# An RWKV time-mixing kernel: adding the mixes of two units in one instruction, and issuing the last three staged loads one unit sooner

## The chip, the cores and the metric

The kernel runs on one core of a Trainium2 chip. The metric is the device time of one execution in microseconds (us), as the median of several runs. Beside it there is a profile of one execution, taken by the hardware profiler; its span runs from the first to the last instruction of the program.

The engines are named as in the profile: PE is the matrix engine (PEld its weight loads), DVE the vector engine, ACT the scalar engine, POOL the GpSimd engine, SP the engine that issues most DMAs. POOL and ACT issue some DMAs too.

## The reference

The input is `x`, 16 batches of 2048 tokens with 256 features, in float32. For each token the kernel mixes it with the token before it, projects the mix twice, and combines the two results:

```
x_prev[:, 1:] = x[:, :-1]                 # zero at the first token of a batch
xv = x * time_mix_v + x_prev * (1 - time_mix_v)
xr = x * time_mix_r + x_prev * (1 - time_mix_r)
v  = xv @ value_weight                    # 256 x 256
r  = xr @ receptance_weight               # 256 x 256
out = (sigmoid(r) * v) @ output_weight    # 256 x 256, float32
```

The reference also makes a mix and a projection for `k`, but its output doesn't use them, and the kernel leaves them out.

## The kernel before

**Units.** The 16 x 2048 tokens are cut into NU = 64 units of 512 tokens, four to a batch. In the transposed layout (features on the partitions) a unit's mix is a tile of 128 x 1024 bf16. The kernel folds `time_mix` into the weights, so that a mix is `c * x_prev + x` with one factor `c = 1/time_mix - 1` per feature: a scaling, and then an add. `m = 0` stands for the receptance mix and `m = 1` for the value mix. The features are held as two halves, `ko = 0` and `ko = 1`.

**The loop.** The main loop runs over g = 0 to 62. Its iteration g does, for unit g, on PE: `project(ps_r, g, 0)` (four matmuls into `psum_r`), the eight transposes of unit g + 6 into `ps_t` while units are still transposed on PE (up to unit 39), `project(ps_v, g, 1)` (four matmuls into `psum_v`), and `output` for an earlier unit (eight matmuls into `psum_o`). For g above 32 the output belongs to unit g - 2 and stands ahead of the value projection. ACT takes the sigmoid of `psum_r` into `s_sb`, copies the transposes out and copies `psum_o` to the output tile. DVE multiplies `s_sb` by `psum_v` into `z_sb`. In what follows r(g), v(g), o(g) are the three groups of matmuls of unit g, and z(g) is that multiplication. `psum_v` has one buffer only (`bufs=1`), so v(g + 1) can't begin until z(g) has read v(g).

**The mixes.** They are made ahead of the projections. From unit 10 (`PAIRS`) on the scaling is done for two units at once (128 x 1024 for one half of the features): DVE scales `ko = 0` (`scale`, L334), POOL scales `ko = 1` (`scale_pool`, L344), and late in the kernel ACT scales `ko = 0` of the value mixes (`scale_act`, L609). The add is done unit by unit on DVE (`add`, L356, 128 x 1024). The lists `products`, `pooled`, `sums` and `held`, built at L577 to L604, say what each iteration issues. DVE's order in iteration g is: the scaling in `products[g]`, the adds in `sums[g]`, z(g), the adds in `held[g]`. Before the change `sums[g]` holds the add of the value mix of unit g + 1, and `held[g]`, behind z(g), the add of the receptance mix of unit g + 2. POOL's scaling in iteration g is made to wait for the last add of `sums[g]`:

```
        for p in pooled[g]:
            wrap_slots(p, after=last)
            scale_pool(p, last)
```

**Order.** The program order is the one written: the kernel turns the automatic scheduling off, and each engine executes its instructions in that order. `wrap_slots` copies one slot of the transposed tile (L528) at each fourth unit.

**Loads and transposes.** Units 0 to 39 (batches 0 to 9) are loaded with a cast to bf16 and transposed on PE. Batches 10 to 15 are staged as bf16 in DRAM (`x_natural`), by loads on POOL's queue, and come into SBUF by two DMA transposes on SP's queue, `by_dma` (L251): batches 10 to 12 at g = 27, batches 13 to 15 at g = 39 (`T_AT`). The loads of batches 13, 14 and 15 are issued at the end of the iterations in `STAGE_AT`, behind POOL's scaling of that iteration. They wait until the first DMA transpose has landed; the second one waits for the last of them. Some stores are held back so that they don't run beside a transpose (`FIRST`, `WAITING`). A store of two units is 1 MB.

Of the kernel before, what the change touches and what calls it, by code (L numbers as in the profile page):

```python
# [15 lines left out]
def kernel(  # L16
# [32 lines left out]
    TU = UJ * P  # L49
# [8 lines left out]
    CROSS = NU - BYDMA - LOOK  # L58
# [3 lines left out]
    FIRST = {21: 27, 27: 39, 29: 39}  # L62
    WAITING = {23: 27, 25: 27, 31: 39, 33: 39, 35: 39}
    ZEROS_AT = 12
    STAGE_AT = {33: 13, 34: 14, 35: 15}
    GROUPS = [(2, 3), (4, 5, 6), (7, 8, 9), (10, 11, 12), (13, 14, 15)]
    HALVED = (12, 15)
    PAD = 16
# [4 lines left out]
    PAIRS = 10  # L73
# [63 lines left out]
    def zero_rows(b, k):  # L137
        rows = zeros[k * PAD : (k + 1) * PAD].rearrange("p (o c) -> p o c", o=1)
        nc.gpsimd.dma_start(
            out=x_both[b][k, :PAD].rearrange("p (h c) -> p h c", c=P),  # L140
            in_=rows.to_broadcast([PAD, KO, P]),
        )

    def load(b):
        if b < STAGED:
            x_bf[b] = xpool.tile([P, J, D], BF16, name="x_bf")
        if b < BYUNIT:
            for e in range(UB):
                nc.gpsimd.dma_start(
                    out=x_bf[b][:, e * UJ : (e + 1) * UJ, :], in_=unit_rows(x, b, e)[:, 0]  # L150
                )
            return
        if b in HALVED:
            return [
                nc.gpsimd.dma_start(out=x_bf[b][:, j : j + J // 2], in_=rows(b)[:, j : j + J // 2])
                for j in (0, J // 2)
            ]
        run = 8192 if b < LONG else 16384
        return nc.gpsimd.dma_start(out=x_bf[b], in_=rows(b), max_dma_last_dim=run)  # L159
# [339 lines left out]
    def tile_for(b):  # L499

        if b not in mix:
            mix[b] = mixpool.tile([P, 2, 2 * UJ, KO, P], BF16, name="mix")

    def pieces(g):

        b, e = divmod(g, UB)
        tile_for(g // 2)
        return [(b, m, e * TU, (e + 1) * TU) for m in range(2)]
# [68 lines left out]
    sums = {g: [] for g in range(-1, NU)}  # L577
# [4 lines left out]
    first = {}  # L582
    held[0].append(pieces(1)[1])
    pooled[0].append(pieces(1)[1])
    for u in range(2, NU):
        p0, p1 = pieces(u)
        if u - 1 <= AHEAD:
            sums[u - 1].append(p0)
        else:
            held[u - 2].append(p0)  # L590
        (held if u - 1 < AHEAD else sums)[u - 1].append(p1)
        first[u] = (u - 1 if u - 1 <= AHEAD else u - 2, u - 1)
# [24 lines left out]
    for g in range(NU - 1):  # L617
# [48 lines left out]
        n = TU // 2 if g == NU - 2 else TU  # L666
# [10 lines left out]
        if ZEROS_AT <= g < ZEROS_AT + len(pads):  # L677
            zero_rows(*pads[g - ZEROS_AT])
        if g in STAGE_AT:
            b = STAGE_AT[g]  # L680
            loads[b] = load(b)
# [40 lines left out]
```

## Time and profile before

| what | value |
|---|---|
| median of 3 runs | 200.81 us (199.84 to 201.69) |
| profiled execution, its own time | 201.01 us |
| span of the profile | 199.2 us |
| PE busy | 192.5 us (97%) |
| DVE busy | 184.4 us (93%), 289 instructions |
| ACT busy | 177.0 us (89%) |
| POOL busy | 86.9 us (44%) |
| DMA | 58.13 MB, mean 292 GB/s |
| DVE adds `mix<-mix,xt_both` (L356), 128 x 1024 | 112, 701 ns each |
| DVE multiplications z (L668), 128 x 1024 | 62, 1216 ns each |
| POOL scalings (L344), 128 x 1024 | 54, 1122 ns each |

Busy times are unions of records. The records of neighbouring instructions on one engine overlap by some tens of ns, so the time that an instruction takes up on its engine is read from the start of one to the start of the next, which is shorter than its record. A busy PE isn't PE at its peak, and an idle gap matters only on an engine that others wait for.

### The profile page before, as it was taken

The page shows a single profiled execution, that of the slowest core. Times are in us where ns is not written, and L with a number is a line of the kernel's source. Part 1 is how long each engine was busy: PE and PEld are TensorE (multiplying, and loading weights), DVE is VectorE, ACT ScalarE, POOL GpSimd, SP SyncE. Part 2 cuts the span into 40 slices and gives each one's busy share as a digit, 9 for nine tenths or more (in the row PEclk, how much of TensorE's full clock was granted, in tenths as well). Part 3 has the DMA queues.
Part 4 walks back from the last instruction along what each step waited for, and adds up shares of the span by engine and source line. Part 5 has one row for each costly group of instructions (what it writes and reads, how often), then busy time and mean ns, then how long its engine had stood idle before and what let it go on. Part 6 is the DMA issues. An engine that isn't in the chain of part 4 may idle for free.

```text
span 199.2 us, 3758 instructions
## 1 busy us (share of the span) xinstructions
PE 192.5 (97%) x1368; PEld 123.5 (62%) x1368; DVE 184.4 (93%) x289; ACT 177.0 (89%) x197; POOL 86.9 (44%) x115
## 2 busy tenths in 40 slices
PE   8999999999999999999999999999999999999990
PEld 3555676666666666666666556666666666666660
DVE  0899999999999999999999999999999999999960
ACT  3699899999999999999999999999999999999970
POOL 1656452453675635524424366444444444444200
PEclk9999999999999999999999999999999999999998
DMA  5799999999999999999999999999999999999994
GB/s 177 203 187 215 215 280 275 278 282 274 286 312 332 285 285 331 296 268 211 296 250 290 367 276 207 209 280 295 198 238 346 416 421 400 409 399 407 409 392 177
DMA packets 37961, 58.13 MB, mean 292 GB/s; under 512 B 26068, under 2 KB 27448, under 8 KB 35128
## 3 DMA queue, kind: packets, MB, share of 16 engines
q1 hardware_dynamic: 33392, 41.34, 60.7%
q0 software_dynamic: 4400, 16.44, 41.6%
q8 instruction: 10, 0.16, 0.3%
q10 hardware_dynamic: 152, 0.13, 0.2%
q14 instruction: 7, 0.06, 0.1%
HBM read 34.34 MB, written 39.90 MB: 373 GB/s over the span
## 4 chain that ended last, share of the span: by engine, by line
PE 88%; ACT 4%; DMA 2%; issue 2%; DVE 1%; SPq 0%; DVEq 0%
PE psum_v L364 26%; PE psum_o L393 26%; PE psum_r L364 26%; PE ps_t L269 8%; DMA w_f<-n_receptance_weight_dram 2%; ACT xt_first L286 1%; ACT s_sb L629 1%; PE psum_r L378 1%; PE ps_t L393 1%; ACT mix L609 1%; ACT o_sb L442 1%; PE ps_t L364 0%; SPq L171 0%; DVE z_sb L668 0%; DVE mix L356 0%
## 5 line engine op out<-in xcount | busy, mean ns | idle before, releaser
L344 POOL TENSOR_SCALAR mix<-xt_both,c_sb 128x1024 bf16<-128x1024 bf16 (+1 forms) x55 | 61.3, 1114 | 84.7 <-DVE mix L356 82.8
L356 DVE TENSOR_TENSOR mix<-mix,xt_both 128x1024 bf16<-128x1024 bf16 x112 | 77.4, 701 | 1.4
L668 DVE TENSOR_TENSOR z_sb<-s_sb,psum_v 128x1024 bf16<-128x1024 bf16 (+1 forms) x64 | 76.7, 1200 | 1.9 <-PE psum_v L364 0.8
L364 PEld LDWEIGHTS <-w_bf 128*128 128x128 bf16 x516 | 49.0, 98 | 38.7 <-DVE mix L356 0.5
L629 ACT ACTIVATE s_sb<-psum_r 128x1024 bf16<-128x1024 f32 x63 | 65.2, 1035 | 6.2 <-PE psum_r L364 6.0
L364 PE MATMUL psum_v<-mix,w_bf 128*128 128x512 bf16 (+1 forms) x256 | 65.3, 377 | 0.1
L364 PE MATMUL psum_r<-mix,w_bf 128*128 128x512 bf16 (+1 forms) x252 | 64.2, 377 | 0.0
L393 PE MATMUL psum_o<-wo_bf,z_sb 128*128 128x256 bf16 x486 | 63.4, 273 | 0.2 <-DVE z_sb L668 0.2
L393 PEld LDWEIGHTS <-z_sb 128*128 128x128 bf16 x512 | 51.7, 103 | 18.2 <-DVE z_sb L481 0.7
L442 ACT COPY o_sb<-psum_o 128x1024 f32<-128x1024 f32 x50 | 51.2, 1024 | 5.0 <-PE psum_o L393 5.0
L286 ACT COPY xt_both<-ps_t 128x1024 bf16<-128x1024 bf16 x32 | 32.8, 1036 | 0.0
L269 PEld LDWEIGHTS <-x_bf 128*128 128x128 bf16 x304 | 19.7, 98 | 8.9 <-DMA x_bf<-in_x_dram 1.5
L269 PE MATMUL ps_t<-ident,x_bf 128*128 128x128 bf16 x304 | 22.7, 219 | 0.3 <-DMA x_bf<-in_x_dram 0.3
L334 DVE TENSOR_SCALAR mix<-xt_both,c_sb 128x1024 bf16<-128x1024 bf16 (+1 forms) x47 | 21.1, 458 | 0.0
L609 ACT ACTIVATE mix<-xt_both,c_sb 128x1024 bf16<-128x1024 bf16 x14 | 16.3, 1161 | 0.0
L356 DVE TENSOR_TENSOR mix<-mix,xt_first 128x1024 bf16<-128x1024 bf16 x15 | 10.6, 713 | 0.1
L442 ACT COPY x_bf<-psum_o 128x1024 f32<-128x1024 f32 x10 | 10.2, 1015 | 0.0
L334 DVE TENSOR_SCALAR mix<-xt_first,c_sb 128x512 bf16<-128x512 bf16 x22 | 6.5, 348 | 0.3 <-ACT xt_first L279 0.2
L286 ACT COPY xt_first<-ps_t 128x1024 bf16<-128x1024 bf16 x6 | 6.2, 1027 | 0.0
L159 POOL DMA_DIRECT2D x_bf<-in_x_dram x8 | 5.7, 712 | 0.0
L528 POOL COPY xt_first<-xt_first 128x254 bf16<-128x254 bf16 x5 | 2.0, 395 | 6.6 <-DVE mix L356 6.6
L344 POOL TENSOR_SCALAR mix<-xt_first,c_sb 128x512 bf16<-128x512 bf16 x6 | 4.1, 689 | 0.7 <-DVE mix L356 0.2
(70 smaller groups left out, 54.0 us busy)
## 6 DMA issues: line engine op xcount, KB each, us to landing
out_dram<-o_sb SPq DMA_DIRECT2D x24, 1024.0 KB, 14.1
x_bf<-in_x_dram POOLq DMA_DIRECT2D x8, 1024.0 KB, 20.6
x_natural<-in_x_dram POOLq DMA_DIRECT2D x4, 1024.0 KB, 13.3
out_dram<-x_bf SPq DMA_DIRECT2D x4, 1024.0 KB, 13.1
x_natural<-in_x_dram POOLq DMA_DIRECT2D x4, 512.0 KB, 15.2
x_bf<-in_x_dram POOLq DMA_DIRECT2D x6, 256.0 KB, 6.1
out_dram<-x_bf SPq DMA_DIRECT2D x6, 256.0 KB, 4.2
o_sb<-in_x_dram SPq DMA_DIRECT2D x4, 256.0 KB, 4.0
```

Source lines behind the costliest of these rows:

```text
L159: return nc.gpsimd.dma_start(out=x_bf[b], in_=rows(b), max_dma_last_dim=run)
L269: nc.tensor.transpose(out=ps[:, jj], in_=src[:, jj, ko * P : (ko + 1) * P], identity=idn)
L286: nc.scalar.copy(out=xt[b][:, j0 : j0 + UJ], in_=ps)
L334: nc.vector.tensor_scalar(out=mixed(piece)[:, :, ko], in0=tokens(piece, 0, ko), scalar1=c_sb[:, m, ko : ko + 1], scalar2=None, op0=ALU.mult,)
L344: op = nc.gpsimd.tensor_scalar(out=mixed(piece)[:, :, 1], in0=tokens(piece, 0, 1), scalar1=c_sb[:, m, 1:2], scalar2=1.0, op0=ALU.mult, op1 ...
L356: return nc.vector.tensor_tensor(out=mixed(piece), in0=mixed(piece), in1=tokens(piece, 1), op=ALU.add)
L364: nc.tensor.matmul(out=ps[:, mo, :], lhsT=w_bf[:, m, ko, mo * P : (mo + 1) * P], rhs=mixed((b, m, e * TU + lo, e * TU + hi))[:, :, ko], st ...
L393: nc.tensor.matmul(out=ps[:, j, :], lhsT=slot[:, ko, j], rhs=wo_bf[:, ko, :], start=(ko == 0), stop=(ko == KO - 1),)
L442: nc.scalar.copy(out=o[:, j0 : j0 + UJ, :], in_=ps)
L609: nc.scalar.activation(out=mixed(piece)[:, :, ko], in_=tokens(piece, 0, ko), func=ACT.Copy, scale=c_sb[:, m, ko : ko + 1],)
L629: nc.scalar.activation(out=s_sb, in_=ps_r, func=ACT.Sigmoid)
L668: nc.vector.tensor_tensor(out=z_sb[:, :, c : c + n], in0=s_sb[:, :, c : c + n], in1=ps_v[:, :, c : c + n], op=ALU.mult,)
```

## The change

For units 12 to 35 the adds are made for two units at once. For each even unit u in that range one add of 128 x 2048 covers the receptance mixes of u and u + 1, in `sums[u - 2]`, and one covers their value mixes, in `sums[u - 1]`. Both stand ahead of the z of their iteration; `held` gets nothing for these units. The 48 single adds of these 24 units go, and 24 double ones come, so that DVE has 24 instructions fewer. Units up to 11 and from 36 on keep the old lists.

The loads of batches 13, 14 and 15 are issued at the end of iterations 32, 33 and 34 and no longer 33, 34 and 35. On POOL's queue each thereby moves ahead of one scaling.

```diff
-    STAGE_AT = {33: 13, 34: 14, 35: 15}
+    STAGE_AT = {32: 13, 33: 14, 34: 15}
...
     for u in range(2, NU):
         p0, p1 = pieces(u)
+        if PAIRS + 2 <= u < CROSS + 2:
+            if u % 2 == 0:
+                for n, (b, m, lo, hi) in ((2, p0), (1, p1)):
+                    sums[u - n].append((b, m, lo, hi + TU))
+            first[u] = (u - 2, u - 1)
+            continue
         if u - 1 <= AHEAD:
             sums[u - 1].append(p0)
         else:
             held[u - 2].append(p0)
         (held if u - 1 < AHEAD else sums)[u - 1].append(p1)
         first[u] = (u - 1 if u - 1 <= AHEAD else u - 2, u - 1)
```

Iteration 10 stands at the border: its `sums` holds the single add of the value mix of unit 11, from the old lists, and then the double add of the receptance mixes of units 12 and 13. Iteration 34 stands at the other one: its `sums` is empty.

## The prediction

> **What bounds the kernel now.** I read first the slices of the page, then the stretches, then the timelines of DVE and PE around unit 10, where the new adds begin, and last the stores at the end.
>
> ```profile
> PE   8999999999999999999999999999999999999990
> DVE  0899999999999999999999999999999999999960
> DMA  5799999999999999999999999999999999999994
> ```
>
> PE, DVE and the DMA engines are all nearly full, so a saving on DVE alone may buy nothing. The table by stretches (busy time of PE, PEld, DVE, ACT, POOL, then the clock, the DMA share, GB/s) says how full:
>
> ```profile
> 40.00:45.00 5.00, 5.00 (x39) 3.29 (x37) 4.90 (x8) 5.00 (x6) 2.94 (x6) 1.00 1.05 281
> ...
> 112.00:134.00 22.00, 22.00 (x138) 13.31 (x136) 21.88 (x32) 20.53 (x23) 11.04 (x12) 1.00 1.01 259
> ...
> 151.00:186.00 35.00, 35.00 (x218) 22.47 (x217) 34.87 (x49) 32.56 (x35) 14.97 (x14) 1.00 1.03 405
> 186.00:199.20 13.20, 7.99 (x58) 5.16 (x56) 6.77 (x11) 6.73 (x13) 0.00 (x0) 0.93 0.82 315
> ```
>
> PE has no idle time at all from 25 us to 186 us: a unit takes 3.05 us with transposes, 2.60 us without, and no wait on DVE is left to take out. DMA is at a share of 1.0 too. At the end the DMA engines drain stores. The view of the output tensor gives, for the store issued at 171.3 us and for the last two, issued at 194.4 and 195.1 us:
>
> ```profile
> DMA to landing us min/median/max: 14.1/14.1/14.1
> ...
> DMA to landing us min/median/max: 3.0/3.0/3.0
> ```
>
> A backlog of stores shrinks towards the end and is almost gone with the last one, which is copied on DVE at 194.18 + 0.43 = 194.6, issued at 195.1 and lands at 198.1. So two limits meet there, PE and the stores.
>
> **What the Trainium skill says.** (1) "VectorE: DVE Perf Modes", section "The TRN2 errata", says that the fixed latency is paid once per instruction, so a larger tile pays it once; the table of tiers in that page keeps a bf16 `tensor_tensor` at 2 elements a cycle. The trace agrees with the fixed part: adds that follow one another start 0.60 us apart, and 1024 elements at 2 per 0.96 GHz cycle are 0.53 us. (2) "SBUF", section "SBUF: two separate sides", says that an add of two SBUF inputs on DVE and a POOL instruction that reads SBUF exclude each other for a whole instruction. The trace agrees: POOL's scaling ends at 42.54 and the add begun at 42.30 takes 0.78 us, not 0.69. (3) "Perfetto Trace Analysis", section "Matmuls", wants matmul groups to rotate through PSUM banks so that the evacuation of one overlaps the next. `psum_v` can't: one buffer. In the trace v(10) starts 0.08 us after the record of z(9) ends. (4) "DMA: Bandwidth & Descriptors", section "Anatomy of one DMA", gives a fixed 2.0 us and the bytes at 436 GB/s; as an estimate from it a store of 128 KB alone lands after 2.3 us. The last one took 3.0, so it had about 0.7 us of backlog before it.
>
> **The change part by part.**
>
> *DVE's saving.* Two adds take 2 x 0.60 = 1.20 us. A double one is not in the trace. Upper bound 1.20 (nothing shared); lower bound 1.07 (its elements alone). I take 0.53 x 2 + 0.07 = 1.13. 24 of them save 24 x 0.07 = 1.7 us of DVE. Against it stands that each double add follows the scaling it depends on: in iteration 9 such an add starts 0.58 us after the scaling (39.98 to 40.56), where an independent one starts after 0.40 (43.00 to 43.40). Before, half of the iterations pay that, now all. DVE's unit is then 0.58 + 1.13 + 1.13 (z) = 2.84, up to 0.1 for POOL's lock and 0.14 for the slot copy in each fourth unit: 2.97 against PE's 3.05. It fits, and it is worth nothing, as no PE wait ends with a DVE add there.
>
> *The border at unit 10.* Here is the cost. DVE, and then PE:
>
> ```profile
> 41.17 1.21 DVE L668 TENSOR_TENSOR z_sb<-s_sb,psum_v 128x1024 bf16<-128x1024 bf16 x1
> 42.30 0.78 DVE L356 TENSOR_TENSOR mix<-mix,xt_both 128x1024 bf16<-128x1024 bf16 x1
> 43.00 0.47 DVE L334 TENSOR_SCALAR mix<-xt_both,c_sb 128x1024 bf16<-128x1024 bf16 x1
> 43.40 0.68 DVE L356 TENSOR_TENSOR mix<-mix,xt_both 128x1024 bf16<-128x1024 bf16 x1
> 44.00 1.21 DVE L668 TENSOR_TENSOR z_sb<-s_sb,psum_v 128x1024 bf16<-128x1024 bf16 x1
> ```
>
> ```profile
> 42.46 1.03 PE L364 MATMUL psum_v<-mix,w_bf 128*128 128x512 bf16 x4
> ...
> 45.06 0.61 PE L269 MATMUL ps_t<-ident,x_bf 128*128 128x128 bf16 x8
> 45.50 1.03 PE L364 MATMUL psum_v<-mix,w_bf 128*128 128x512 bf16 x4
> ```
>
> The rows are z(9), the late add of unit 11's receptance mix, the scaling for 12 and 13, the add of unit 11's value mix, z(10). DVE is behind already: v(10) ends at 43.49 and z(10) starts at 44.00. The change puts a double add ahead of z(10), in the one iteration that still has both single adds: z(10) starts at 44.00 + 1.13 = 45.13 and ends at 46.34; v(11), due at 45.50, starts at 46.42. Behind it in PE's queue stands everything else. Cost: 0.92 us of PE, once. Nothing hides it; PE has no gap to give back.
>
> *After it.* z(10) is followed by the scaling, which POOL's lock (scaling 45.3 to 46.4) holds to 46.4, the double add at 46.98, z(11) from 48.1 to 49.3; v(12) is due at 46.42 + 3.05 = 49.47. It fits by 0.15 us, and each unit wins about 0.1 back. POOL's scaling starts when the add before it ends and takes 1.12 us, while DVE does z and a scaling (1.71), so it is ready for the next double add.
>
> *The other border, unit 34.* Iteration 34 loses its add ahead of z(34), and DVE waits for PE some 1 us. From z(35) on, the order is the old one. No gain: PE is the bound.
>
> *The loads.* Three issues of about 0.56 us each on POOL move ahead of one scaling each. Load 13 can't go before the first transpose has landed, at 99.0 + 13.7 = 112.7, against 115.0 before. POOL waits there about 1 us at most; queued behind is the scaling of iteration 33, which itself waits for an add that ends near 114, so it is hidden (if not, the add that reads it comes 3 us later). Load 14 goes from 117.8 to about 116, load 15 from 120.2 to about 118.
>
> ```profile
> 99.00 11.61 SPq L251 DMA_TRANSPOSE xt_both<-x_natural  x1
> ...
> 133.90 17.23 SPq L251 DMA_TRANSPOSE xt_both<-x_natural  x1
> ```
>
> The second transpose waits for load 15, landing at 120.7 + 13.0 = 133.7. In this stretch the DMA share is 1.01: the loads share the engines with 2 MB of stores, and an earlier issue shifts the bytes but doesn't shrink them. I take 0.3 us gained at the start of the transpose; bounds 0 and 2 (a real idle gap, which no slice shows).
>
> *The end.* PE is 0.9 later: the last copy ends at 195.5. The stores have had 0.9 us more to drain and began up to 0.3 earlier, so the 0.7 of backlog and part of the 0.46 between copy and issue go. 195.5 + 0.2 + 2.4 = 198.1 to 198.4, against 198.1. Net +0.2 us. The profiled execution's 201.01 becomes 201.2; it stood 0.2 above the median of 200.81, so the median becomes 201.0.
>
> **The rivals.**
>
> *A, the stall is passed on in full* (201.7). If a store alone takes 3.0 us anyway, the tail gives nothing back: 200.81 + 0.92. For it: the landing times at the end flatten out at 3.0. Against it: the very first load, 256 KB in an idle start (0.75 to 3.5 us), took 2.75, and 128 KB has half the bytes.
>
> *B, the loads matter* (200.1). If the transpose starts 1 to 2 us sooner, the backlog ends sooner, the tail shrinks by its 0.7, and with a smaller stall than mine the net is -0.7. Against it: the DMA share of 1.01. For more than 1% PE too would have to end 2 us sooner, and it has no idle time.
>
> *C, slower: DVE no longer fits in PE's unit* (203.6). Place: units 11 to 35. Price: if a double add costs more than 1.21 from start to start, DVE's unit exceeds 3.05 and the lag never heals; each z frees `psum_v` late. At 1.33 that is 0.12 x 23 = 2.8 on top of 0.9, less 0.9 that the tail absorbs: +2.8. It decides from about 1.29, where the sum passes 2 us. For it: the margin is only 0.08 a unit, and POOL's lock may cost more than 0.1. Against it: the fixed part is paid once.
>
> *D, the change does not do what it says*: in the changed program's own order of instructions DVE has 24 fewer, with the double adds where I put them, so this gets no chance.
>
> **How the numbers follow.** My forecast 0.60, A 0.16, B 0.14, C 0.10. 1% (2 us) is about what a measurement of this kernel can tell from no change; its three runs spread over 0.9%. My forecast, A and nearly all of B lie within 1%: same 0.86. Slower by over 1% is C, 0.10; faster is the outer end of B, 0.04. The range runs from B, 200.0, to a mild C, 202.3.
>
> **What would show it.** Right: DVE has 24 adds of 128x2048 with records near 1.22 us; PE shows one gap near 0.9 us before v(11), put down to DVE, and none later; the stretches of 15 us after it are full; load 13 is issued near 112.8, the second transpose between 133.3 and 134.5; the last stores land in less than 3.0 us. Wrong: gaps of PE before many v between 48 and 112 us (C); no gap at 45.5 us; a second transpose before 132.5 us (B); or last stores that still take 3.0 us (A).

## The result, and the profile after

| | median | range | runs |
|---|---|---|---|
| before | 201.03 us | 199.37 to 202.15 | 22 |
| after | 200.22 us | 199.64 to 201.79 | 22 |

The ratio is 0.9974 with a 95% interval of 0.9955 to 0.9993, so the change saves 0.5 us (0.1 to 0.9); the two medians of the table lie 0.8 apart, inside that interval. I had forecast 201.0, no change or 0.2 us more. The profiled execution of after took 200.22 us, with a span of 198.4 us (before 201.01 and 199.2).

The slices of the page look almost as before:

```profile
PE   8899999998999999999999999999999999999992
DVE  1899999999999999999999979999999999999972
DMA  5999999999999999999999999999999999999985
```

What is new on PE stands in the tenth slice (its 8), and DVE's idle time in the 24th (the first 7). PE's waits in all:

```profile
PE psum_r L378 <- DVE w_prev L549: 0.9, 1, 0.9
PE ps_t L201 <- PEq L712: 0.8, 1, 0.8
PE psum_v L364 <- DVE z_sb L674: 0.7, 1, 0.7
PE psum_o L393 <- DVE z_sb L674: 0.2, 1, 0.2
PE ps_t L269 <- DMA x_bf<-in_x_dram: 0.2, 1, 0.2
```

Each row gives us in total, times, and the longest. The third is the only wait on DVE in the main loop, and it comes once. The first two and the last belong to the head of the program, the fourth to its end; before has these four kinds too. The wait is the one at the border, read in the timeline of DVE and then of PE:

```profile
43.13 1.81 DVE L356 TENSOR_TENSOR mix<-mix,xt_both 128x1024 bf16<-128x1024 bf16 x2
44.87 1.21 DVE L674 TENSOR_TENSOR z_sb<-s_sb,psum_v 128x1024 bf16<-128x1024 bf16 x1
46.00 0.47 DVE L334 TENSOR_SCALAR mix<-xt_both,c_sb 128x1024 bf16<-128x1024 bf16 x1
46.58 1.23 DVE L356 TENSOR_TENSOR mix<-mix,xt_both 128x2048 bf16<-128x2048 bf16 x1
47.72 1.22 DVE L674 TENSOR_TENSOR z_sb<-s_sb,psum_v 128x1024 bf16<-128x1024 bf16 x1
```

```profile
42.19 1.03 PE L364 MATMUL psum_v<-mix,w_bf 128*128 128x512 bf16 x4
...
46.13 1.02 PE L364 MATMUL psum_v<-mix,w_bf 128*128 128x512 bf16 x4 [0.73 <-DVE z_sb L674]
```

The row "x2" of 1.81 us joins the single add and the double one, and z(10) stands behind both. v(11) was due at 42.19 + 3.05 = 45.24 and starts at 46.13, 0.9 late; the trace puts 0.73 of it down to z(10). So PE loses what I said it would. The gain is elsewhere: on SP's queue and in the stretch of the second DMA transpose. These are the rows of the transpose in after, and then the stretch of 134 to 152 us of before and of after (the columns are those of the prediction's table; the last one is GB/s):

```profile
134.25 15.31 SPq L251 DMA_TRANSPOSE xt_both<-x_natural  x1
```

```profile
134.00:152.00 18.00, 18.00 (x112) 11.54 (x111) 17.91 (x25) 16.37 (x19) 7.86 (x7) 1.00 1.18 254
```

```profile
134.00:152.00 18.00, 18.00 (x113) 11.43 (x111) 17.90 (x25) 16.37 (x18) 7.84 (x7) 1.00 1.19 288
```

The transpose starts 0.35 us later than before (134.25 against 133.90), and its issue takes 15.31 us and not 17.23. SP is free for the next store at 149.6 and not at 151.1. In the same 18 us the DMA engines move 288 GB/s and not 254, at the same busy share. That lead lasts to the end, where the last stores of after, five of them issued after 193 us, show:

```profile
L411 SPq DMA_DIRECT2D out_dram<-x_bf x4: 332/338/410, 193.7 to 195.3; - x4
...
DMA to landing us min/median/max: 2.0/2.0/2.0
```

In before the five stores issued after 193 us took 3.0 to 3.6 us, and the groups of DMA issues on the page tell the same of the larger ones: the median store of 256 KB now lands after 2.5 us, and took 4.2. So the stores are no longer behind. The last copy ends at 194.81 + 0.42 = 195.23, its store is issued at 195.26 without a wait, and lands at 197.26; before it was 194.61, 195.07 and 198.06.

### The profile page after: what moved, and what is told of

Its sections match the earlier page's. It is cut to its first block, busy times and chain, and to the rows that moved or that the text cites. A ratio compares the mean times of both kernels' runs of the same rounds, so it can differ in the third digit from the quotient of the medians.

```text
span 198.4 us, 3734 instructions
## 1 busy us (share of the span) xinstructions
PE 191.7 (97%) x1368; PEld 122.7 (62%) x1368; DVE 183.0 (92%) x265; ACT 176.9 (89%) x197; POOL 87.1 (44%) x115
## 4 chain that ended last, share of the span: by engine, by line
PE 74%; DVE 16%; issue 3%; DMA 2%; ACT 1%; POOL 1%; SPq 0%; DVEq 0%; POOLq 0%
PE psum_v L364 22%; PE psum_o L393 22%; PE psum_r L364 22%; DVE mix L356 6%; DVE z_sb L674 5%; PE ps_t L269 5%; DVE mix L334 4%; DMA w_f<-n_receptance_weight_dram 2%; PE ps_t L393 1%; PE psum_r L378 1%; ACT xt_first L279 1%; ACT s_sb L635 1%; PE ps_t L364 0%; SPq L171 0%; POOL x_bf L159 0%
## 5 line engine op out<-in xcount | busy, mean ns | idle before, releaser
L356 DVE TENSOR_TENSOR mix<-mix,xt_both 128x1024 bf16<-128x1024 bf16 (+1 forms) x88 | 72.3, 835 | 2.5
```

The source lines that it names most:

```text
L356: return nc.vector.tensor_tensor(out=mixed(piece), in0=mixed(piece), in1=tokens(piece, 1), op=ALU.add)
```

## The experiments

Every ratio below is to the kernel before, run beside the other on the same chip.

### Which part, and what sets the end

One theory (L in the texts) was that the sooner loads bring the gain, the other (S) that by themselves they don't. The first two runs do one part of the change alone: the loads alone,

```diff
-    STAGE_AT = {33: 13, 34: 14, 35: 15}
+    STAGE_AT = {32: 13, 33: 14, 34: 15}
```

> The loads of batches 13 to 15 one unit sooner, nothing else of the change. Theory L (the gain comes from the loads: they let the second DMA transpose and the stores behind it finish sooner, so that PE and not the stores sets the end; the double adds only cost 0.9 us of PE at unit 11): faster than before by 1.0 to 1.6 us, near 199.5, and faster than the changed kernel by 0.5 to 0.9 us; PE without a gap at v(11); last store landing 2.0 us after its issue. Theory S (the gain comes from the double adds, by fewer DVE instructions and so other times of instruction fetches beside the transposes): same as before, 201.0 within 0.3 us, second transpose of 16 to 17 us, last stores 3.0 us.

Measured: 201.17 us, ratio 0.9977 (0.9947 to 1.0007). The interval holds 1, so the run alone decides nothing, but a saving of more than 1.1 us it excludes. Its profile (POOL, DVE and PE around 115 us) shows a price that the loads can have without the double adds:

```profile
115.05 0.56 POOL L159 DMA_DIRECT2D x_natural<-in_x_dram  x1 [3.66 <-DVE z_sb L668]
115.65 1.12 POOL L344 TENSOR_SCALAR mix<-xt_both,c_sb 128x1024 bf16<-128x1024 bf16 x1
```

```profile
115.20 1.85 DVE L334 TENSOR_SCALAR mix<-xt_both,c_sb 128x1024 bf16<-128x1024 bf16 x1
116.97 0.68 DVE L356 TENSOR_TENSOR mix<-mix,xt_both 128x1024 bf16<-128x1024 bf16 x1
117.58 1.21 DVE L668 TENSOR_TENSOR z_sb<-s_sb,psum_v 128x1024 bf16<-128x1024 bf16 x1
```

```profile
118.84 1.02 PE L364 MATMUL psum_v<-mix,w_bf 128*128 128x512 bf16 x4 [1.10 <-DVE z_sb L668]
```

The view puts POOL's wait down to z, but load 13 is issued 0.53 us after the landing of the first transpose, as in after. That landing came late in this execution, at 114.52: in six of the 14 profiles it is recorded 2.0 us after the last packet of the transpose and not 0.5 us, and why isn't known. POOL's scaling behind the load starts 0.6 us after it, at 115.65. There it runs beside DVE's scaling, which takes 1.85 us and not 0.47. z(34) comes late and PE loses 1.1 us. So in this profile load 13 is no sooner than in before (115.00); loads 14 and 15 are 1.1 and 1.4 us sooner. In after load 13 goes at 113.15 and DVE has 1 us to spare in iteration 34, so nothing is lost.

The double adds alone, with the old loads:

```diff
+        if PAIRS + 2 <= u < CROSS + 2:
...
+            continue
```

> The double adds for units 12 to 35, with the loads at their old places. Theory L: no faster than before, 201.0 to 201.9, as PE loses 0.9 us at v(11) and the stores still end late. Theory S: as fast as the changed kernel, near 200.2, although PE loses the same 0.9 us at v(11); second transpose near 15.3 us.

Measured: 200.61 us, 0.9969 (0.9947 to 0.9991): as much as the whole change. The stall at v(11) is there (0.7 us on PE), the issue of the second transpose takes 15.92 us, and the last store lands 2.0 us after its issue. So the gain needs no sooner load, although the adds touch neither the loads nor the transposes.

What the end is worth, I tested from both sides. First a stall at the same place without the change: three extra DVE adds of 128 x 512 ahead of z(10).

```diff
+        if g == 10:
+            for n in range(3):
+                nc.vector.tensor_tensor(out=idle[:, n], in0=wo_bf, in1=wo_bf, op=ALU.add)
```

> The kernel before with three more adds of 128 x 512 on DVE ahead of z(10), into a tile that nobody reads: they make v(11) wait about 0.8 us, as the double add does in the changed kernel, and change nothing else. If the stores set the end of the kernel before (the view in both theories), PE's 0.8 us are absorbed: 201.0 within 0.3 us. If PE sets the end in most runs, it is 0.8 us slower, 201.8.

Measured: 201.56 us, 1.0027 (1.0004 to 1.0050), which is +0.5 us (0.1 to 1.0). The stall came out larger than meant, 1.44 us at v(11) in the trace, and about a third of it shows: the end takes up the rest, and the last store again lands in 2.0 us.

Then less to store: before without the 1 MB store of units 30 and 31, whose rows of the output are left unwritten. At the 405 GB/s that the prediction's table shows from 151 us on, 1 MB is about 2.6 us of the DMA engines' time.

```diff
+            elif g == 31:
+                pass
```

> The kernel before without the 1 MB store of units 30 and 31 (that part of the output is left unwritten): 2.4 us less for the DMA engines behind the second transpose, nothing less for PE. If the stores set the end of the kernel before, it falls to where PE sets it: last store landing 2.0 us after issue, 199.3 to 199.7 us, 1.3 to 1.7 faster than before. If PE sets the end, less than 0.4 us faster.

Measured: 199.58 us, 0.9909 (0.9884 to 0.9933): 1.8 us less, though PE's work is the same and the second transpose is as slow as in before (18.09 us). So the stores, not PE, set the end of before. A sum puts both together: when PE sets the end, it is the last copy of before, 194.61, plus the stall, plus 0.03 to the issue, plus 2.0. With no stall that is 196.6, 1.4 less than before's 198.06; with 0.92 it is 197.56, 0.5 less, which is what after gained. With the 1.44 of the extra adds it is 198.08, no loss; that kernel measured 0.5 (0.1 to 1.0), so the sum is good to about half a microsecond.

### Why the second transpose got shorter

The traces of the first runs held a candidate (F), an instruction fetch. The page lists, beside the queues of the kernel's own DMAs, this one:

```profile
q14 instruction: 7, 0.06, 0.1%
```

Seven packets of 8 KB. "DMA: Bandwidth & Descriptors", section "Queues, rings and completion order", of the Trainium skill says that row 14 belongs to the runtime, refills among its uses; that q14 is this row is my reading. The packet records of the trace give the times. Two of the seven change place between the kernels: 86.8 and 147.9 us in before, 93.5 and 160.7 in after; the others stay within 1.3 us. DVE's stream is the one that the change shortens (24 instructions), so I take the two for fetches of DVE's instructions; the profile doesn't name them. (The page has a second row of this kind, q8, with ten packets of 16 KB. None of them falls between the first and the last packet of the second transpose, in any of the 14 profiles.) At 147.9 the second transpose runs, at 160.7 it doesn't. Stretches of one microsecond in before:

```profile
147.00:148.00 1.00, 1.00 (x6) 0.49 (x5) 1.00 (x3) 1.00 (x2) 0.17 (x1) 1.00 1.30 297
148.00:149.00 1.00, 1.00 (x11) 0.89 (x10) 1.00 (x2) 1.00 (x2) 0.96 (x1) 1.00 1.74 110
149.00:150.00 1.00, 1.00 (x7) 0.48 (x5) 1.00 (x2) 1.00 (x2) 0.00 (x0) 1.00 0.91 205
```

A steady 290 to 297 GB/s falls to 110 and recovers: the packets of the transpose are in flight, the busy share rises to 1.74, and they don't move. In after the same stretch reads

```profile
148.00:149.00 1.00, 1.00 (x8) 0.57 (x6) 1.00 (x2) 1.00 (x2) 0.54 (x1) 1.00 1.28 290
```

The size: from packet 6000 of the transpose to packet 12000 it takes 5.29 us without such a fetch and 6.20 to 6.22 with one, in 13 of 14 profiles; in the last one the fetch falls just before packet 6000, and the same 0.9 us are missing there. So such a fetch costs the transpose 0.92 us: the eight profiles with one have such a hole, which begins within half a microsecond of the fetch's start, and the six without have none. If F is right, DVE instructions that do nothing but fill move the hole. The fills are `nc.vector.memset` of one column. In after, 23 of them bring the count nearly back:

```diff
+    FILL = {**{g: 1 for g in range(14, 33)}, 33: 4}
...
+        for n in range(FILL.get(g, 0)):
+            nc.vector.memset(idle[:, 4 * g + n : 4 * g + n + 1], 0.0)
```

> The changed kernel with 23 tiny fills of 128 x 1 on DVE (one in each of iterations 14 to 32, four in iteration 33), which nobody reads: about as many DVE instructions as the double adds took away, in slack that DVE has. Theory F (instruction fetch: with fewer DVE instructions the fetch of DVE's next 8 KB of instructions moves from inside the second DMA transpose, 147.9 us, to behind it, 160.7 us; inside, it stops the transpose for about 1 us): the fetch comes back to about 148 us, the transpose shows a hole of 0.9 to 1.0 us just after it and takes 16 us or more, and the gain over before is lost: 201.0 to 201.4. Theory L (the gain comes from the loads and the work of DVE, not from where a fetch falls): as the changed kernel, 200.2 to 200.6.

Measured: 200.63 us, 0.9974 (0.9954 to 0.9994), no loss against after. The fetch came at 149.9 and the hole from 150.4 to 151.3:

```profile
149.00:150.00 1.00, 1.00 (x9) 0.86 (x8) 1.00 (x2) 1.00 (x2) 1.00 (x1) 1.00 1.30 297
150.00:151.00 1.00, 1.00 (x6) 0.48 (x5) 1.00 (x2) 1.00 (x2) 0.06 (x1) 1.00 1.71 122
```

So the fills do move the hole, but the time missed its forecast: the last stores still landed in 2.0 us. The transpose lost 0.9 us and the stores weren't late. That fits the sum above, in which PE, with its stall, sets the end of after.

The other way round, 28 fills in before (two in each of the iterations 17 to 30) should bring the fetch ahead of the transpose, and 8 (one in each of 17 to 24) should leave it inside, as a control for the fills' own cost.

> The kernel before with 28 tiny fills of 128 x 1 on DVE, two in each of iterations 17 to 30: more instructions, no double adds, loads at their old places. Theory F: the fetch moves ahead of the second transpose, to about 132 us; no hole in it, 15 to 16 us; the end is set by PE in most runs: 199.5 to 200.3, faster than before by 0.8 to 1.5, as PE has no gap at v(11). Theory L: no faster than before.

> The control for the 28 fills: the kernel before with 8 of them, one in each of iterations 17 to 24. The fetch moves by about 4 to 5 us only, to 143 us, still inside the second transpose. Theory F: as before, within 0.4 us, with the hole near 144 us. If tiny fills help for another reason: faster by about 0.3 of what the 28 bring.

Measured: with 28 fills 200.76 us, 0.9972 (0.9944 to 1.0000), fetch at 132.9 (and an eighth packet on q14, at 193.2), no hole; with 8 fills 201.63 us, 1.0013 (0.9992 to 1.0035), fetch at 145.8 and the hole behind it at 146. But the transpose with 28 fills, expected at 15 to 16 us, was hardly shorter than in before:

```profile
134.03 17.03 SPq L251 DMA_TRANSPOSE xt_both<-x_natural  x1
```

Its first 2000 packets took 4.4 us (3.8 in before), and its last stores landed after 2.6 us or more. So the hole moves as F says and the fills cost nothing that shows, but this pair does not show that moving it saves time: the profile misses the forecast, and each interval touches 1.

### Taking the stall away

If PE sets the end of after, it should gain from a border without the stall. In this version, shown against after, no iteration near unit 10 gets a double add on top of a single one: the doubles begin at unit 16, for the value mixes first, and for the receptance mixes at unit 20; the units 16 to 19 keep single receptance adds.

```diff
-        if PAIRS + 2 <= u < CROSS + 2:
+        if PAIRS + 6 <= u < CROSS + 2:
...
-                    sums[u - n].append((b, m, lo, hi + TU))
+                    if m or u >= PAIRS + 10:
+                        sums[u - n].append((b, m, lo, hi + TU))
+            if u < PAIRS + 10:
+                (held if u % 2 else sums)[u - 2].append(p0)
```

> The changed kernel with a gentler border: double adds of the value mixes from units 16 and 17 on, of the receptance mixes from units 20 and 21 on; for units 16 to 19 the receptance mix of the even unit is added ahead of z, of the odd unit behind it. 18 DVE instructions fewer than before, loads one unit sooner. By the sum of starts z is never more than 0.5 us late, so PE has no gap on DVE between 25 and 186 us. Theory F: the fetch falls near 157 us, behind the transpose: PE's 0.9 us are won, 199.3 to 199.7. If instead the stall is not what the changed kernel loses: 200.2.

Measured: 199.85 us, 0.9949 (0.9929 to 0.9968): 1.0 us less than before, the lowest time of all that computes everything. Its interval overlaps that of after (0.9955 to 0.9993), so that it beats after is likely but not shown. From 25 to 192 us its profile has a single wait of PE:

```profile
PE psum_o L393 <- DVE z_sb L677: 0.2, 1, 0.2
```

and the transpose is the short one, 15.31 us:

```profile
133.53 15.31 SPq L251 DMA_TRANSPOSE xt_both<-x_natural  x1
```

This version has no stall to cover a late store, so it can tell what each cause of the shorter transpose is worth. Once with the old loads, and once with the new loads and 22 fills that put the fetch back into the transpose:

> The kernel with the gentler border, but the loads of batches 13 to 15 at their old places. If the loads matter for how fast the second transpose gets going (its first 1000 packets took 1.6 to 2.0 us in four profiles with sooner loads and 2.2 to 3.9 in six with old ones): 2.2 us or more for them and slower than with sooner loads by 0.3 to 0.8 us, 200.2 to 200.7. If only the double adds matter: 199.85, within 0.3 us.

> The kernel with the gentler border and sooner loads, with 22 tiny fills of 128 x 1 on DVE (one in each of iterations 16 to 32, five in iteration 33) that bring DVE's instruction fetch from 157 us back to about 147 us, into the second transpose. Theory F: a hole of 0.92 us in the transpose, whose issue takes 16.2 us, not 15.3; PE's end is at 196.3 in this kernel, so 0.2 to 0.9 us of it show in the time: 200.1 to 200.7. If the fetch costs nothing: 199.85, within 0.2 us.

Measured: 200.47 us, 0.9966 (0.9946 to 0.9986), with the old loads; 200.64 us, 0.9981 (0.9959 to 1.0002), with the fetch at 146.8. The transposes (old loads, then the fetch):

```profile
134.85 15.99 SPq L251 DMA_TRANSPOSE xt_both<-x_natural  x1
```

```profile
133.94 16.67 SPq L251 DMA_TRANSPOSE xt_both<-x_natural  x1
```

and the hole of the second one, together with its last stores:

```profile
147.00:148.00 1.00, 1.00 (x6) 0.46 (x5) 1.00 (x3) 1.00 (x2) 0.01 (x1) 1.00 1.57 88
```

```profile
DMA to landing us min/median/max: 2.8/2.8/3.0
```

With the old loads the last stores land in 3.0 us. So with either one put back the stores are late again. By the ratios the loads are worth 0.3 us here and the fetch 0.6 (the medians, from two chips, would say 0.6 and 0.8); the intervals overlap, so the times settle neither size. The profiles don't isolate the two causes fully either. The first transpose happened to land at 114.5 and 114.0 us in them, against 112.0 in the version that they are compared with, and the second one starts 1.3 and 0.4 us later. Its last packet is 2.0 and 1.8 us later; the slower beginning is 0.7 us of this with the old loads, and the hole 0.9 us with the fetch.

Last, the two kernels again:

> The kernel before once more, for its profile alone: the instruction fetch at 147.5 to 149 us, and a hole of 0.92 us in the second transpose behind it (theory F says always); 2.2 us or more for the first 1000 packets of the transpose, if these hang on the loads; last stores 2.7 to 3.0 us where the transpose takes 17 us or more.

> The changed kernel once more, for its profile alone: the fetch at 160 to 161 us, no hole in the second half of the second transpose; 1.6 to 2.0 us for its first 1000 packets, if these hang on the loads; PE's gap of 0.7 to 0.9 us at v(11); last stores 2.0 us.

Before: 201.72 us, transpose 17.99 us, fetch at 147.6 with its hole, the last stores landing after 2.6 to 4.5 us. After: 200.38 us, transpose 15.42 us, fetch at 160.7, 0.7 us lost at v(11), last stores 2.0 us. The picture holds.

The sooner loads go with a quicker beginning of the transpose. Its first 2000 packets take 2.5 to 3.0 us in five of the six profiles with sooner loads and 3.4 to 4.8 us in the eight with the old ones; the sixth, the loads alone, takes 3.7. From there on the pace is the same everywhere, but for the hole. The beginning also varies between executions of one kernel (3.8 and 4.8 us in the two profiles of before). Why it is quicker stays open. It shares the engines with two stores that were held back for it. The second of these lands 1.3 to 1.7 us after the transpose's first packet in the six profiles with sooner loads, and 1.8 to 3.6 us after it in the eight with the old ones; packet 2000 follows that landing by 1.2 to 1.8 us in all but two (the loads alone and the 28 fills, 2.2 and 2.6). So the beginning mostly takes as long as that store does, but no run moves the store alone, and why it lands sooner isn't shown.

## Why the prediction was wrong

Point by point:

- *The double add.* 1.13 us from start to start was the estimate; 46.58 to 47.72 is 1.14. Right, and so was C's price, which this excludes: no wait of PE on DVE follows v(11) until the end. The 0.78 us that I put down to POOL's lock agree only roughly: an add held from 42.30 to 42.54 and then taking 0.69 would take 0.93. The scaling of 1.85 us in the run with the loads alone shows the two engines in each other's way more clearly.
- *The border.* 0.92 us lost at v(11), once, nothing hides it on PE: 0.9 measured. Right. That z(34) waits about 1 us for PE is right too (1.02).
- *The loads at their issue.* Load 13 at 113.15 (forecast 112.8), with POOL waiting 0.79 us, hidden. Right for after. The run with the loads alone shows what the cover is: the spare microsecond that the double adds leave in iteration 34.
- *The loads' worth: the step that failed.* I wrote "0.3 us gained at the start of the transpose". I priced the start alone and took the duration as given, because the bytes stay the same. It was the other way round: the start came 0.35 us later, and the issue took 1.9 us less. Of this, 0.92 us is the packet on q14, by my inference a fetch of DVE's instructions, which the double adds move out of the transpose. I counted 24 fewer instructions as DVE time (1.7 us, worth nothing) and not as a place in an instruction stream; with the old loads too, the double adds alone bring the issue to 15.92 us. The rest, 1.0 us, is the quicker beginning that goes with the sooner loads and whose cause stays open. None of the views that the prediction reads shows either; the row of 110 GB/s at 148 us would have shown the first.
- *The end.* I had the sum as 195.5 + 0.2 + 2.4, with 2.4 near the estimate of 2.3 us from "DMA: Bandwidth & Descriptors", section "Anatomy of one DMA", of the Trainium skill. That section's figures are for DMAs issued from POOL, and these stores are issued from SP and ACT, so the estimate was borrowed from another path. The measured terms are 0.03 and 2.0: the backlog is not almost gone but gone, because SP is free for the stores 1.6 us sooner (149.62 and not 151.18). That is 0.6 us less than I took. The copy ended at 195.23, for the head of this execution happened to be 0.27 us earlier (v(10) at 42.19 and not 42.46).

So the terms that were mis-sized all belong to the stores: the transpose ahead of them was 1.9 us shorter and not equal, and with that the 0.2 + 2.4 at the end became 0.03 + 2.0, which turns +0.2 into -0.5. Rival B had the direction and nearly the time (200.1), but not the mechanism: it wanted a transpose that starts 1 to 2 us sooner. Rival A falls with the last stores' 2.0 us.

## What to carry to other kernels

When two limits meet at the end of a kernel, price a change on both: a stall on the engine is paid only after the stores' backlog is used up, and a shorter transfer in the middle pays only if no such stall was added. Price a moved transfer by its whole duration and by what runs beside it, not by its start alone; look for single slices in which the GB/s fall while the DMA share rises. And where a change alters the number of instructions on an engine, look in the trace where the packets of the instruction queues fall, since they move too.

## What was unexpected of the hardware

- One 8 KB packet on queue 14 during a DMA transpose stops the transpose for 0.92 us, the same within 0.02 us in all eight profiles that have one. That queue's seven packets hold 0.1% of the DMA time, and so look like nothing on the page.
- Which engine such a fetch serves was inferred from the fetches that move: 24 DVE instructions fewer shift it from 147.9 to 160.7 us, 28 more to 132.9, 8 more to 145.8.
- A store of 128 KB without a backlog landed 2.0 us after its issue from SP or ACT, below the 2.3 us of the prediction's estimate (worked out from figures for DMAs of POOL) and below the 3.0 us that it takes behind others in before.
